# Hybrid SSD and chunk-MLP block on one core: four small products and a hold issued later, residual additions on VectorE, and another order of the last tiles

## The chip, the cores and the metric

The kernel runs on 1 core of one Trainium2 chip. The metric is the device time in microseconds of one execution. A core has TensorE (PE, matrix products into PSUM), VectorE (DVE), ScalarE (ACT), GpSimd (POOL) and SyncE (SP), whose queue issues the DMA transfers. Each engine works through its own instructions in the order in which the program issued them, and waits on semaphores for what others produce.

## What is computed

One transformer-like block on 1152 rows of width 1024: 1024 rows of one prompt and 128 rows of eight running streams. In the reference, cut to what matters here:

```python
h = rms_norm(x, norm_g[0]) * (1 + sc1) + sh1
z, xbc, dt_raw, uv = jnp.split(h @ w_in, ...)
xbc_act = silu(causal_conv(xbc))              # split into xs, B, C
dt = softplus(dt_raw + dt_bias)
y = ssd_scan(xs, dt, A, B, C, h0) + d_skip * xs
y_ssd = rms_norm(y * silu(z))
u, v = split(gelu(uv)); v = layer_norm(v)
y_cmlp = u * (tril(w_s) @ v + b_s)            # chunks of 128 rows
m = concat(y_ssd, y_cmlp) @ w_out
x = x + g1 * rms_norm(m, norm_g[1])
h = rms_norm(x, norm_g[2]) * (1 + sc2) + sh2
f = square(relu(h @ w_ff1)) @ w_ff2
x = x + g2 * rms_norm(f, norm_g[3])
```

All of it is in float32, and states and caches are returned too.

## The kernel before

The 1152 rows are nine tiles of 128 rows (t = 0 to 8), in three groups of three (g = 0, 1, 2; GT = 3, GW = 384 rows). Float32 products are made of three passes: each operand is split into a high part (a cast) and a low part (a subtraction). A split is a cast on ScalarE (L238, L258) or VectorE (L240) and a subtraction on VectorE (L241, L259); weights are split by a cast (L317, L319) and a subtraction L326 on GpSimd or VectorE, and the low part is kept in DRAM (`kl`) and loaded again as `wl` for later groups.

The mixer goes through the groups in order. `prep1_task(g)` loads x in natural and in transposed form, takes the sum of squares, scales the transposed tile by r (a small product `pr`, L506, spreads r over the partitions; L507 multiplies), modulates it (L427 on ScalarE; L433 and L434 on VectorE for tile 8) and splits it into `hT`. `m_in(g)` then runs the input projection: eight column tiles `xbc_0` to `xbc_7` with the convolution behind each (L632 to L656), then z in two halves (`pz0`, `pz1`), u in four column tiles (`pu_0` to `pu_3`) and v in two halves (`pv0`, `pv1`). `m_out(g)` is the output projection (`wo`, L1006 to L1009), and `out_task(g)` puts the residual on M, tile by tile. `ssd_task(g)` is the scan: gates of dt (L764 to L790, ending in `dA`), a prefix product `pa` (L797), its negative `nac` on VectorE (L805) and the transpose `pn` (L813), from which `rr` is built (L825), and per tile `px`, `pbn`, `par` (L859 to L879), the decays L (L892), `yd`, `yo`, `su` (L897 to L912). The MLP follows: `prep2_first` and others scale M by r (L456, L470), transpose it (`pt`, L252) and split it; then come the first products, with W made of sums of weights and of activations, and the long second product from 600 us to the end.

What sets the order is written out by hand. `m_in` and `m_out` are the main sequence; the small tasks are Python generators that stand in lanes. A lane runs one task at a time, in the order in which they were added. Each time the main sequence has issued some matmuls, it advances a model clock by their estimated ns, and a task goes on when the wait that it last gave has run out on that clock. These waits are the table WAIT: `dA0` is the wait of group 0 ahead of `pa`, `yd0` that ahead of `yd`, `prep1_tr1` and `prep1_tr2` those of groups 1 and 2 ahead of the first `pr`. `finish(task)` issues all that is left of a task before the main sequence goes on. `prep1_task(g)` waits for another task ahead of its first write to `hT`; for g = 2 that is `ssd_task(1)`:

```python
            if tl == 0:
                while not after.done:
                    yield
                new_hT(g)
```

In `m_in`, `ssd_task(g)` is added to lane A behind pz0. In `out_task` the tile's M is multiplied by r and the gate on VectorE (L1043) and the residual is added by `eng("xr")`, GpSimd (L1044). In `m_f2` the last pass ends with a loop over the three last tiles (L1704 on): per tile the rest of the product, a sum (L1713), ScalarE's square of one half (`fin_half`, L1633), the sum of both halves (L1637, `fin_r`) and r on GpSimd, then the product with r and gate (`fin_mul`, L1645), the addition to `x1l` (`fin_add`, L1651) and the store.

Of the kernel before, what the change touches and what calls it, by code (L numbers as in the profile page):

```python
# [19 lines left out]
D = 1024  # L20
KD = 8
NT = 9
GT = 3
# [18 lines left out]
def shape_constants():  # L42
# [14 lines left out]


WAIT = dict(
    L=12100, L0=3200, L1=0, L2=400, dA=28300, dA0=2400, dA1=2800, dA2=3200, evac=4100, gs1=4100, h0=4100, ln=5900,  # L60
    ln0=7300, ln1=9100, ln2=10000, lnr=5600, lnr0=2800, lnr1=600, lnr2=2000, modB=3000, modC=7600, mod_gate=2000,
    mod_load=8200, mod_mt=2100, next8=0, nexttile=6700, nexttile0=800, nexttile1=2400, nexttile2=1900, pn=20800,
    pn0=1900, pn1=0, pn2=3800, prep1_load=17400, prep1_load1=1700, prep1_load2=3200, prep1_next=13800,
    prep1_next1=4400, prep1_next2=1000, prep1_norm=11500, prep1_norm1=3300, prep1_norm2=800, prep1_split=40000,
    prep1_split1=400, prep1_split2=1000, prep1_stat=6500, prep1_stat1=1000, prep1_stat2=0, prep1_tr=5600,
    prep1_tr1=0, prep1_tr2=3500, prep2_load=1700, prep2_load0=200, prep2_load1=1500, prep2_load2=3600,
    prep2_next=3200, prep2_next0=2800, prep2_next1=2500, prep2_next2=5000, prep2_norm=6200, prep2_norm0=4000,
    prep2_norm1=3500, prep2_norm2=5000, prep2_split=1700, prep2_split0=1200, prep2_split1=800, prep2_split2=1500,
    prep2_stat=9600, prep2_stat0=1500, prep2_stat1=2500, prep2_stat2=4500, rr=11700, rr0=800, rr1=13000, rr2=400,
    set_load=10000, set_pcc=0, set_pw=2900, sp=13000, sp0=800, sp1=500, sp2=1900, sp_mid=22500, sp_mid0=9600,  # L70
    sp_mid1=0, sp_mid2=1400, sz=20900, sz0=1300, sz1=800, sz2=0, x1=14700, x10=2500, x11=7200, x12=4700, xr=29300,
    xr0=3000, xr1=2600, xr2=2700, yT=45700, yT0=2500, yT1=5600, yT2=2800, yc=23700, yc0=15400, yc1=16900,
    yc2=9500, yd=400, yd0=4500, yd1=6000, yd2=4900, yo8=2500, yr=11700, yr0=200, yr1=0, yr2=1100)
ENG = dict(p1hi=1, p2hi=0, ychi=0, yc=1, xdt=1, xw=1, xnD=1, L0=0, L1=0, sp=0, vg=0, vb=1, xr=1, S=0, rr=0, sz=1)
LO_POOL = {0, 1, 6, 7, 8, 9, 10, 11, 12, 13, 14, 15, 16, 17, 18, 19, 20, 21, 22, 24, 25, 26, 27, 28, 31, 32, 33, 35, 36, 39, 40, 41, 42, 43, 44, 46, 52, 53, 54, 55, 56, 60, 63, 64, 66, 68, 70, 72, 73, 77, 79, 80, 83, 85, 87, 89, 90, 91, 92, 93, 94, 95, 96, 97, 98, 100, 102, 103}
LOADS = [
# [41 lines left out]
def tile_block(ctx, tc, io, out):  # L118
# [13 lines left out]
    def eng(key):  # L132
        return pool if ENG[key] else dve
# [57 lines left out]
    def finish(*tasks):  # L191
        for t in tasks:
            while not t.done:
                tick(500.0)
# [504 lines left out]
    def m_in(g, ct0=0):  # L699
        if g not in gA:  # L700
            new_gA(g)
        dtx[g] = const.tile([P, GT, 8], F32, tag="dtx", name=f"dtx{g}", bufs=2)
        yT[g] = [None, None]

        def ev_u(ct):
            return lambda a: gelu2(up[g][:, ct, :], a[:, 0:GW], GW, f"gu{g}{ct}")

        def ev_z(half):
            def f(tl, a):
                if half == 0:  # L710
                    dve.tensor_tensor(dtx[g][:, tl, :], a[:, 0:8], dtb, op=ALU.add)
                a = a[:, 8:264] if half == 0 else a[:, 0:256]
                th = gt(f"zt{g}{tl}{half}")
                act.activation(th, a, AF.Tanh, scale=0.5)
                dve.scalar_tensor_tensor(sz[g][:, tl, 256 * half:256 * half + 256], th, 1.0, a, op0=ALU.add, op1=ALU.mult)
                zdone[g] = tl + GT * half
            return f

        for ct in range(ct0, 8):
            yield from m_proj_b(g, f"xbc{g}_{ct}", lambda a, ct=ct: xbc_evac(g, ct, a))  # L720
        if g > 0:
            finish(*gm_tasks[g - 1])
        if g == 2:
            finish(*out_tasks[0], p0)
        sz[g] = fslot(1 + g % 2, [P, GT, 512], F32, f"sz{g}")
        up[g] = fslot(0, [P, 4, GW], F32, f"up{g}")
        yield from m_proj_a(g, 264, f"pz0{g}", ev_z(0))
        ssd_tasks[g] = laneA.add(ssd_task(g))
        yield from m_proj_a(g, 256, f"pz1{g}", ev_z(1))
        for ct in range(4):  # L730
            yield from m_proj_b(g, f"pu{g}_{ct}", ev_u(ct))
        if g > 0:
            finish(ssd_tasks[g - 1])
        finish((mod_tasks[g] if g < 2 else ssd_tasks[1]))
        vall = fslot(1 + (g + 1) % 2, [P, GT, 512], F32, f"vt{g}")
        yT[g][1] = slot(YB_SLOT[g], [P, 4, 2, GW], F32R, f"yTb{g}")
        gm_tasks[g] = []

        def ev_v0(tl, a):
            gelu2(vall[:, tl, 0:256], a[:, 0:256], 256, f"gv0{g}{tl}")  # L740

        def ev_v1(tl, a):
            gelu2(vall[:, tl, 256:512], a[:, 0:256], 256, f"gv1{g}{tl}",
                  lambda: gm_tasks[g].append(laneG[tl].add(gmlp_task(g, tl, vall[:, tl, :]))))

        yield from m_proj_a(g, 256, f"pv0{g}", ev_v0)
        yield from m_proj_a(g, 256, f"pv1{g}", ev_v1)
        flush()
# [272 lines left out]
    def out_task(g, sst, ready):  # L1021
# [17 lines left out]
        for tl in range(GT):  # L1039
# [1 line left out]
            gv = gs1 if t == 8 else gate[0]  # L1041
            m = M[g][:, tl, :]
            dve.scalar_tensor_tensor(m, m, r, gv, op0=ALU.mult, op1=ALU.mult)  # L1043
            eng("xr").tensor_tensor(m, m, xs[tl], op=ALU.add)  # L1044
            if tl + 1 < GT:
                while tl + 1 not in ready:
                    yield
# [633 lines left out]
    def m_f2():  # L1681
# [4 lines left out]
        for i, (an, bn, gn) in enumerate(PASSES):  # L1686
# [20 lines left out]
            if last:  # L1707
                f2_prep(len(jobs2))
                for t in range(GT):
# [3 lines left out]
                    dve.tensor_tensor(a, a, bank[t], op=ALU.add)  # L1713
                    if t == 0:
                        finish(ft, ft2)
                    r = fin_r(GT + t, [fin_half(GT + t, 0), half1[:, t:t + 1]])
                    if t < 2:
                        fin_mul(GT + t, r)
                        fin_add(GT + t, x1l[:, t, :], ((0, 512, dve), (512, D, dve)))
                    else:  # L1720
                        for c0, c1, e in ((0, 384, pool), (384, D, dve)):
                            fin_mul(GT + t, r, ((c0, c1),))
                            fin_add(GT + t, x1l[:, t, :], ((c0, c1, e),))
                    yield 3 * LAST * 230.0
                continue
            if i == 0:
# [89 lines left out]
```

## Time and profile before

| | |
|---|---|
| median of 3 runs | 1334.36 us (1334.32 to 1338.89) |
| the profiled execution | 1334.28 us, span 1332.1 us |
| TensorE (PE) busy | 1254.1 us, 94% |
| VectorE (DVE) busy | 833.4 us, 63% |
| ScalarE (ACT) busy | 629.6 us, 47% |
| GpSimd (POOL) busy | 238.6 us, 18% |
| mean granted TensorE clock | 0.976 of full speed |

The busy shares are averages over stages with different limits. A row of the waits view says how long an engine sat idle ahead of a line, in total, how often, the longest, and what ended it. The columns of the other views stand at their first group below.

### The profile page before, as it was taken

How to read it: one execution, taken by the hardware profiler on the slowest of the kernel's cores; microseconds unless marked ns; L12 is line 12 of the kernel's file. 1: busy time of each engine (PE TensorE's matmuls, PEld its weight loads, DVE VectorE, ACT ScalarE, POOL GpSimd, SP SyncE). 2: the span in 40 equal slices, each digit the busy share in tenths (PEclk: the TensorE clock that was granted, in tenths of full speed). 3: DMA queues.
4: the chain of work that ended last, by engine and by line, in shares of the span. 5: the costliest groups of instructions: out<-in, count | busy, mean ns of one | idle time of the engine just before them, and what ended most of it. 6: DMA issues, size and time to landing. Idle time of an engine off the chain costs nothing. (4 is left out here: it accounts for less than half of the span.)

```text
span 1332.1 us, 18561 instructions
## 1 busy us (share of the span) xinstructions
PE 1254.1 (94%) x6815; PEld 1115.8 (84%) x6815; DVE 833.4 (63%) x1309; ACT 629.6 (47%) x1184; POOL 238.6 (18%) x266
## 2 busy tenths in 40 slices
PE   6988879989979999889999999999999999999996
PEld 4967767878779977789999999999988888888875
DVE  5476789566673543799885467576555335337666
ACT  3445534355574523546755444445433334344551
POOL 0133575147330443330000000000000000000001
PEclk9999979999999999989999999999999999999998
DMA  9778546745776467848448976665898337345863
GB/s 348 260 257 307 184 130 235 258 159 190 279 279 237 170 228 261 324 155 281 152 150 279 325 254 216 228 225 187 289 344 314 135 133 270 135 171 200 325 228 126
DMA packets 107154, 307.31 MB, mean 231 GB/s; under 512 B 12052, under 2 KB 31636, under 8 KB 107064
## 3 DMA queue, kind: packets, MB, share of 16 engines
q1 hardware_dynamic: 106632, 304.52, 64.6%
q10 hardware_dynamic: 432, 1.62, 0.3%
q8 instruction: 53, 0.87, 0.3%
q14 instruction: 37, 0.30, 0.1%
HBM read 232.47 MB, written 73.62 MB: 230 GB/s over the span
## 5 line engine op out<-in xcount | busy, mean ns | idle before, releaser
L241 DVE TENSOR_TENSOR bs<-br,bs 128x512 fp32r<-128x512 f32 x128 | 85.9, 689 | 107.2 <-ACT bs L238 106.9
L238 ACT CAST bs<-br 128x512 fp32r<-128x512 f32 x128 | 77.5, 619 | 146.5 <-PE G L1679 87.9
L1677 PE MATMUL P<-bs,as 128*128 128x512 f32 x336 | 132.1, 393 | 1.1 <-DVE acc L1740 1.1
L1679 PE MATMUL P<-bs,as 128*128 128x512 f32 x336 | 132.0, 393 | 0.0
L1678 PE MATMUL P<-bs,as 128*128 128x512 f32 x336 | 131.7, 392 | 0.0
L245 POOL TENSOR_SCALAR fr<-fss 128x1 f32<-128x1 f32 x9 | 2.8, 314 | 649.4 <-DVE fss L1637 649.4
L241 DVE TENSOR_TENSOR as<-ar,as 128x1536 fp32r<-128x1536 f32 x44 | 77.0, 1757 | 46.5 <-ACT as L238 46.5
L238 ACT CAST as<-ar 128x1536 fp32r<-128x1536 f32 x44 | 64.8, 1478 | 50.3 <-DMA ar<-fdA 26.2
L326 POOL TENSOR_TENSOR wl<-wr,wh 128x1024 fp32r<-128x1024 f32 (+1 forms) x28 | 70.3, 2514 | 86.7 <-ACT wh L319 52.1
L1677 PEld LDWEIGHTS P<-bs,as 128*128 128x128 f32 x336 | 63.1, 188 | 16.4 <-DVE acc L1740 2.0
L1678 PE MATMUL G<-bs,as 128*128 128x512 f32 x192 | 75.3, 392 | 0.0
L1677 PE MATMUL G<-bs,as 128*128 128x512 f32 x192 | 75.2, 392 | 0.0
L1679 PE MATMUL G<-bs,as 128*128 128x512 f32 x192 | 75.2, 392 | 0.0
L1679 PEld LDWEIGHTS P<-bs,as 128*128 128x128 f32 x336 | 63.1, 188 | 14.4
L1678 PEld LDWEIGHTS P<-bs,as 128*128 128x128 f32 x336 | 63.1, 188 | 14.2
L317 ACT CAST wh<-wr 128x1024 fp32r<-128x1024 f32 (+1 forms) x44 | 46.1, 1050 | 44.7 <-PE wo L1007 29.1
L652 DVE SCALAR_TENSOR_TENSOR cva<-pre,cwh,cva 128x256 f32<-128x256 f32 (+1 forms) x78 | 47.7, 653 | 12.4 <-ACT pre L634 11.5
L609 PE MATMUL xbc<-hT,wh 128*128 128x384 f32 x144 | 52.3, 363 | 0.0
L610 PE MATMUL xbc<-hT,wh 128*128 128x384 f32 x144 | 50.7, 352 | 0.0
L1447 DVE TENSOR_TENSOR wt<-wt 128x512 f32<-128x512 f32 x16 | 11.0, 689 | 51.6 <-DMA wt<-in_w_ff_dram 25.0
L1678 PEld LDWEIGHTS G<-bs,as 128*128 128x128 f32 x192 | 36.0, 188 | 8.2
L1677 PEld LDWEIGHTS G<-bs,as 128*128 128x128 f32 x192 | 36.0, 188 | 8.1
(938 smaller groups left out, 3674.0 us busy)
## 6 DMA issues: line engine op xcount, KB each, us to landing
wf<-in_w_f_dram SPq DMA_DIRECT2D x54, 512.0 KB, 4.8
wl<-kl SPq DMA_DIRECT2D x42, 512.0 KB, 4.2
wt<-in_w_ff_dram SPq DMA_DIRECT2D x16, 1024.0 KB, 6.3
td<-wt SPq DMA_DIRECT2D x64, 256.0 KB, 2.9
br<-in_w_ff_dram SPq DMA_DIRECT2D x32, 512.0 KB, 4.6
br<-td SPq DMA_DIRECT2D x32, 512.0 KB, 4.4
kl<-wl SPq DMA_DIRECT2D x26, 512.0 KB, 6.7
wr<-in_w_o_dram SPq DMA_DIRECT2D x24, 512.0 KB, 5.5
```

The costliest lines, as they stand in the source:

```text
L238: act.copy(hi, src)
L241: dve.tensor_tensor(lo, src, hi.bitcast(F32), op=ALU.subtract)
L245: pool.tensor_scalar(r, ss, 1.0 / n, eps, op0=ALU.mult, op1=ALU.add)
L317: act.copy(hi, raw)
L326: (pool if i in LO_POOL else dve).tensor_tensor(lo, raw, hi.bitcast(F32), op=ALU.subtract)
L609: pe.matmul(o, wh[:, k, :], x[:, 0, :], start=k == 0, stop=False)
L610: pe.matmul(o, wh[:, k, :], x[:, 1, :], start=False, stop=False)
L652: dve.scalar_tensor_tensor(dst, tap, w(k), dst, op0=ALU.mult, op1=ALU.add)
L1447: dve.tensor_tensor(b11, b12, b11, op=ALU.subtract)
L1677: pe.matmul(bank, x[:, 0], b[:, 0], start=first, stop=False, skip_group_check=True)
L1678: pe.matmul(bank, x[:, 0], b[:, 1], start=False, stop=False, skip_group_check=True)
L1679: pe.matmul(bank, x[:, 1], b[:, 0], start=False, stop=last, skip_group_check=True)
```

## The change

It does four things. Four entries of WAIT grow: `dA0` from 2400 to 6300, `yd0` from 4500 to 8500, `prep1_tr1` from 0 to 3000 and `prep1_tr2` from 3500 to 6000. In `m_in(2)` the `finish` of group 0's `out_task` and of `p0` (`prep2_first`) is moved from ahead of z to behind pz0. In `out_task` the residual addition of groups 1 and 2 is on VectorE. And in the last tiles both halves of acc are multiplied by the gate ahead of r; behind r one instruction per half multiplies by r and adds to `x1l`, all of it on VectorE.

```diff
-    ... dA=28300, dA0=2400, ...
+    ... dA=28300, dA0=6300, ...
-    prep1_tr1=0, prep1_tr2=3500, ...
+    prep1_tr1=3000, prep1_tr2=6000, ...
-    yc2=9500, yd=400, yd0=4500, ...
+    yc2=9500, yd=400, yd0=8500, ...
@@ m_in
         if g > 0:
             finish(*gm_tasks[g - 1])
-        if g == 2:
-            finish(*out_tasks[0], p0)
         sz[g] = fslot(1 + g % 2, [P, GT, 512], F32, f"sz{g}")
         up[g] = fslot(0, [P, 4, GW], F32, f"up{g}")
         yield from m_proj_a(g, 264, f"pz0{g}", ev_z(0))
+        if g == 2:
+            finish(*out_tasks[0], p0)
         ssd_tasks[g] = laneA.add(ssd_task(g))
@@ out_task
-            eng("xr").tensor_tensor(m, m, xs[tl], op=ALU.add)
+            (pool if g == 0 else dve).tensor_tensor(m, m, xs[tl], op=ALU.add)
@@ m_f2
-                    r = fin_r(GT + t, [fin_half(GT + t, 0), half1[:, t:t + 1]])
-                    if t < 2:
-                        fin_mul(GT + t, r)
-                        fin_add(GT + t, x1l[:, t, :], ((0, 512, dve), (512, D, dve)))
-                    else:
-                        for c0, c1, e in ((0, 384, pool), (384, D, dve)):
-                            fin_mul(GT + t, r, ((c0, c1),))
-                            fin_add(GT + t, x1l[:, t, :], ((c0, c1, e),))
+                    ss = [fin_half(GT + t, 0), half1[:, t:t + 1]]
+                    for cc in (lo, hi):
+                        dve.tensor_tensor(acc[1][:, t, cc], acc[1][:, t, cc], gate[1][:, cc], op=ALU.mult)
+                    r = fin_r(GT + t, ss)
+                    for cc in (lo, hi):
+                        dve.scalar_tensor_tensor(x1l[:, t, cc], acc[1][:, t, cc], r, x1l[:, t, cc], op0=ALU.mult,
+                                                 op1=ALU.add)
+                        load(out=yout(GT + t)[:, cc], in_=x1l[:, t, cc])
```

The four waits move many rows of the mixer. Three places are shown. The first is TensorE's order where group 0's output projection (`wo`) ends and `xbc_0` of group 2 begins; `pr` is the small product that spreads r of a tile of group 2, and the two shown are the second and the third. Rows of `wo` are left out at "...". Before, 66 rows stand between the second `pr` and `xbc_0`:

```order
L506 MATMUL pr_3215<-cs,r_3089 128x128
L1006 MATMUL wo_3059<-wh_3068,yTb_1221 128x512
...
L506 MATMUL pr_3261<-cs,r_3112 128x128
L1006 MATMUL wo_3264<-wh_3125,yTa_1245 128x512
...
L1009 MATMUL wo_3264<-wl_3278,yTb_1221 128x512 x2
L609 MATMUL xbc_0_3382<-hT_3198,wh_3307 128x384
```

And in the change, where 21 are left:

```order
L506 MATMUL pr_3299<-cs,r_3021 128x128
L1006 MATMUL wo_3231<-wh_3210,yTb_1221 128x512
...
L506 MATMUL pr_3350<-cs,r_3063 128x128
L1006 MATMUL wo_3231<-wh_3240,yTb_1221 128x512
...
L1009 MATMUL wo_3231<-wl_3241,yTb_1221 128x512 x2
L609 MATMUL xbc_0_3374<-hT_3285,wh_3273 128x384
```

Both `pr` moved some 45 rows towards `xbc_0`. On VectorE, between the product with the second `pr` and the last split of `hT` (L241), the change has these rows (`yTb` is the split of the gMLP output of group 1, which stood behind `hT` before):

```order
L507 TENSOR_TENSOR xT_3066<-xT_3066,pr_3299 128x1024
L240 CAST yTb_2597<-vt_2596 128x4x128
L241 TENSOR_TENSOR yTb_2597<-vt_2596,yTb_2597 128x4x128
L241 TENSOR_TENSOR hT_3285<-xT_3066,hT_3285 128x4x128
L241 TENSOR_TENSOR hT_3286<-xT_3066,hT_3286 128x4x128
...
L507 TENSOR_TENSOR xT_3291<-xT_3291,pr_3350 128x1024
...
L433 TENSOR_TENSOR xT_3291<-xT_3291,mod_G_108 128x512
L434 TENSOR_TENSOR xT_3291<-xT_3291,mod_sh_107 128x512
...
L241 TENSOR_TENSOR hT_3285<-xT_3291,hT_3285 128x4x128
L241 TENSOR_TENSOR hT_3286<-xT_3291,hT_3286 128x4x128
```

Three pairs L240 and L241 of `yTb` now lie among the rows that `xbc_0` needs.

The third place is TensorE between the u and v columns of group 1. Before, `pa` and `pn` of group 1's scan stand in `pu_0` and `pu_1`, and behind `pu_3` its tiles follow:

```order
L616 MATMUL pu_3_2541<-hT_1142,wl_2449 128x384 x4
L859 MATMUL px_2577<-cs,gA_1508 128x128 x4
L866 MATMUL pbn_2584<-cs,gA_1508 128x128 x2
L868 MATMUL pbn_2584<-gA_1508 128x128 x2
L879 MATMUL par_2592<-rr_2474,lt_2467 128x512
```

In the change:

```order
L616 MATMUL pu_3_2487<-hT_1142,wl_2394 128x384 x4
L797 MATMUL pa_2550<-dA_2548,cs 128x24
L798 MATMUL pa_2550<-dA_2548,nones 128x24
L384 MATMUL pm_2563<-modC_1492,cT 32x512 x4
L813 MATMUL pn_2569<-cs,nac_2556 128x128
L252 MATMUL mt_2585<-cs,modC_1492 128x128 x4
L587 MATMUL pv_0_2604<-wh_2437,hT_1141 128x256
```

The scan of group 1 starts behind `pu_3` there, and its tiles spread over `pv` and into `wo` of group 0.

## Rows read from the trace of the kernel before

**Rows 1.** the page's part 1, busy time, share of the span and instructions

```profile
PE 1254.1 (94%) x6815; PEld 1115.8 (84%) x6815; DVE 833.4 (63%) x1309; ACT 629.6 (47%) x1184; POOL 238.6 (18%) x266
```

**Rows 2.** TensorE's waits: line, what ended them, us in total, times, longest

```profile
PE pt L252 <- DVE M L470: 7.2, 4, 3.5
PE yd L897 <- DVE L L892: 7.2, 6, 4.4
...
PE pr L506 <- POOL r L246: 5.3, 2, 2.9
PE W L1406 <- DVE op2A L1359: 4.1, 1, 4.1
PE pa L797 <- DVE dA L790: 3.9, 1, 3.9
PE pt L252 <- DVE M L456: 3.7, 2, 2.0
PE xbc L616 <- DMA wl<-kl: 3.0, 1, 3.0
```

**Rows 3.** stretches: span, busy PE, PEld, DVE, ACT, POOL, granted clock, DMA

```profile
145.90:149.20 3.30, 3.30 (x12) 3.18 (x12) 2.44 (x8) 1.57 (x7) 0.89 (x3) 0.50 0.96 359
173.20:186.70 13.50, 10.62 (x38) 9.47 (x38) 11.01 (x12) 2.04 (x4) 9.81 (x7) 0.50 0.32 119
...
398.50:405.20 6.70, 5.50 (x25) 5.50 (x26) 1.20 (x4) 4.26 (x10) 0.00 (x0) 0.50 0.28 116
```

**Rows 4.** the same view by stage, of three stages

```profile
141.40:189.00 47.60, 34.75 (x179) 31.67 (x179) 38.67 (x55) 15.86 (x36) 30.06 (x28) 0.82 0.44 146
...
267.40:320.00 52.60, 49.04 (x328) 42.91 (x327) 36.67 (x61) 27.81 (x54) 28.27 (x28) 1.00 0.45 163
...
560.00:600.00 40.00, 33.61 (x172) 31.50 (x171) 36.10 (x51) 21.05 (x47) 11.93 (x12) 0.91 0.52 163
```

**Rows 5.** VectorE's timeline, 160 to 182 us: start, us, line, tiles

```profile
164.75 2.74 DVE L678 TENSOR_TENSOR vt<-vt,vg 128x512 f32<-128x512 f32 x1
167.41 3.61 DVE L652 SCALAR_TENSOR_TENSOR cva<-pre,cwh,cva 128x384 f32<-128x384 f32 x3
```

**Rows 6.** VectorE's timeline, gates of group 1's scan, first and last of 18

```profile
244.85 0.17 DVE L764 TENSOR_SCALAR ab<-dtx 128x24 f32<-128x24 f32 x1
...
249.73 0.18 DVE L790 TENSOR_TENSOR dA<-dt,acol 128x24 f32<-128x24 f32 x1
```

**Rows 7.** TensorE's timeline, two rows of wo with 18 matmuls from one to other

```profile
337.17 0.39 PE L1006 MATMUL wo<-wh,yTa 128*128 128x512 f32 x1
...
341.34 0.39 PE L1006 MATMUL wo<-wh,yTb 128*128 128x512 f32 x1
```

**Rows 8.** VectorE's and ScalarE's timeline, last tiles of prep1(2)

```profile
335.74 3.20 ACT L427 ACTIVATE xT<-xT,mod_sh,mod_G 128x128 f32<-128x128 f32 x8 [1.60 <-DVE xT L507]
...
339.78 1.14 ACT L238 CAST hT<-xT 128x512 fp32r<-128x512 f32 x2
...
343.75 1.21 DVE L507 TENSOR_TENSOR xT<-xT,pr 128x1024 f32<-128x1024 f32 x1
...
348.62 1.47 DVE L241 TENSOR_TENSOR hT<-xT,hT 128x512 fp32r<-128x512 f32 x2
350.00 0.42 DVE L240 CAST yTb<-vt 128x512 fp32r<-128x512 f32 x1
```

**Rows 9.** POOL's and VectorE's timeline, residual addition of tile 6

```profile
571.74 2.39 POOL L1044 TENSOR_TENSOR M<-M,xr 128x1024 f32<-128x1024 f32 x1 [9.35 <-DVE M L1043]
...
571.90 2.52 DVE L241 TENSOR_TENSOR h2T<-M,h2T 128x256 fp32r<-128x256 f32 x1
...
574.65 0.42 DVE L241 TENSOR_TENSOR h2T<-M,h2T 128x256 fp32r<-128x256 f32 x1
```

**Rows 10.** VectorE's timeline, last tiles, first row of two tiles

```profile
1312.78 0.69 DVE L1713 TENSOR_TENSOR acc<-acc,P 128x512 f32<-128x512 f32 x1 [1.75 <-PE P L1679]
...
1317.98 0.68 DVE L1713 TENSOR_TENSOR acc<-acc,P 128x512 f32<-128x512 f32 x1
```

More of the change, by code (lines that the diff above doesn't have):

```diff
@@ L59 @@
 WAIT = dict(
-    L=12100, L0=3200, L1=0, L2=400, dA=28300, dA0=2400, dA1=2800, dA2=3200, evac=4100, gs1=4100, h0=4100, ln=5900,
+    L=12100, L0=3200, L1=0, L2=400, dA=28300, dA0=6300, dA1=2800, dA2=3200, evac=4100, gs1=4100, h0=4100, ln=5900,
     ln0=7300, ln1=9100, ln2=10000, lnr=5600, lnr0=2800, lnr1=600, lnr2=2000, modB=3000, modC=7600, mod_gate=2000,
@@ L65 @@
     prep1_split1=400, prep1_split2=1000, prep1_stat=6500, prep1_stat1=1000, prep1_stat2=0, prep1_tr=5600,
-    prep1_tr1=0, prep1_tr2=3500, prep2_load=1700, prep2_load0=200, prep2_load1=1500, prep2_load2=3600,
+    prep1_tr1=3000, prep1_tr2=6000, prep2_load=1700, prep2_load0=200, prep2_load1=1500, prep2_load2=3600,
     prep2_next=3200, prep2_next0=2800, prep2_next1=2500, prep2_next2=5000, prep2_norm=6200, prep2_norm0=4000,
@@ L72 @@
     xr0=3000, xr1=2600, xr2=2700, yT=45700, yT0=2500, yT1=5600, yT2=2800, yc=23700, yc0=15400, yc1=16900,
-    yc2=9500, yd=400, yd0=4500, yd1=6000, yd2=4900, yo8=2500, yr=11700, yr0=200, yr1=0, yr2=1100)
+    yc2=9500, yd=400, yd0=8500, yd1=6000, yd2=4900, yo8=2500, yr=11700, yr0=200, yr1=0, yr2=1100)
 ENG = dict(p1hi=1, p2hi=0, ychi=0, yc=1, xdt=1, xw=1, xnD=1, L0=0, L1=0, sp=0, vg=0, vb=1, xr=1, S=0, rr=0, sz=1)
```

## The prediction, as it was put on record before the change ran

> **What bounds the kernel.** I read the page's busy shares first, then TensorE's waits grouped by what ended them, then TensorE's rows beside those of VectorE and GpSimd at each place that the change touches. TensorE is busy for 94% of the span [rows 1], and every later stage takes its output, so time is won only where it idles or runs at a low clock. The waits list names places: the transposes of M behind VectorE's L470 (7.2 us, the longest 3.5), yd behind L892 (7.2, longest 4.4), pr behind GpSimd's r (5.3, longest 2.9), W behind op2A (4.1), pa behind dA (3.9), pt behind L456 (3.7), xbc behind a weight load (3.0) [rows 2]. Nearly all stand between 86 and 600 us; the long product from 600 us on hardly waits. A wait has a second price: in the stretches after pa, after yd and after the hold ahead of z the granted clock is 0.50, the 1.2 GHz level instead of 2.4 [rows 3]. The engine had idled just before each of them. A stretch of 3.3 us at half clock costs half its work, 1.65 us, which I add to any TensorE wait of 2 us or more.
>
> The sum is made against the profiled execution, 1334.28 us (span 1332.1), which is the median of the runs, 1334.36, to 0.1 us.
>
> **A. First pr of group 1 (prep1_tr1).** It moves from the middle of pu_0 to its end, behind four pm rows and 16 matmuls, so r is there when it is reached. Removed: the 2.9 us wait [rows 2] and 1.7 of clock. **−4.6**. L507 and the modulation behind it have 24 matmuls of pu_1 and more as cover before hT of group 1 is asked for.
>
> **B. pa and yd of group 0 (dA0, yd0).** The pa row moves past the 24 matmuls of xbc_0, and the yd rows two column tiles on. Between 141.4 and 189 us TensorE works 34.75 of 47.6 us [rows 4]: 12.9 idle. Of the 13.5 us at half clock behind yd 10.62 are busy, so 5.3 are lost, and 1.65 behind pa [rows 3]; some 20 us are at stake. They don't all go. In VectorE's order nac (L805) now stands behind L677, L678, a statistics pair and three conv rows L652, which it did not before, and pn in xbc_1 needs it. Such an L678 took 2.74 us and such a triple of L652 3.61 in that stretch [rows 5]; their 6.3 us are the nearest price, so I put the wait at pn at 6 and add 3 of clock. What mix and su wait for, 2.9 us with 2.5 of clock, is VectorE's own backlog (38.67 busy of 47.6) and stays. 20 less 9 less 5.4 is 5.6: **−6**; from −12 (pn in time) to +2 (the backlog takes all back).
>
> **C. Group 1's scan, next in the same lane, starts later.** A lane runs one task at a time, so ssd_task(1) begins when ssd_task(0) has ended. Its gates were issued before pu_1, with pu_0 as cover; now they stand behind pu_3, and pa is the first row behind it, with only pm, pn and mt left until pv_0. VectorE's gate rows run from 244.85 to 249.91 [rows 6], 5.1 us, and the last gelu row before them takes another 0.5 behind pu_3; the new wait at pa is about 5.4, at pn and mt together 1.1, and 1.7 of clock: 8.2. The stretch from 267.4 to 320 us works 49.04 of 52.6 us [rows 4]: 3.6 us of short waits among the scan's rows, nearly all (I take 3.3) at this place, go with the rows that moved away. Net **+4.9**; 0 if the gates are picked up earlier than the order suggests, +9 if those short waits come again at pv.
>
> **D. First pr of group 2 (prep1_tr2).** It moved too; its 2.4 us (the rest of the 5.3 of [rows 2]) and 1.7 of clock go. **−4.1**.
>
> **E. Entry into group 2.** This is the bill for C and D. prep1(2) may write hT only when ssd_task(1) is done, so the second and third pr fall from 66 and 50 rows ahead of xbc_0 to 21 and 5. Behind the second pr 24 matmuls of wo remain; 18 of them take 4.17 us [rows 7], so the cover is 5.6. The chain that must end first: pr 0.4, L507 1.2, L427 3.2, the copies L238 0.6 and a wait for ScalarE's other rows 1.5, two L241 1.5, one pair L240 and L241 1.1, L507 1.2, another such pair 1.1, four L433/L434 (of L241's shape, 0.7 each) 2.8, L238 0.6, L241 0.7 [rows 8]. That is 16 us; with L241 at the longer times that it has beside GpSimd's wl it is 19. The wait at xbc_0 is 10.4 to 13; I take 11.2 and 3 of clock: **+14.2**; from +9.7 to +20.
>
> **F. What that wait gives back.** Weight loads for group 2 go on while TensorE stands. The wait of xbc for wl, 3.0 with 1.7 of clock, should vanish, and half of the 2.0 at L456 with 0.9 of clock. **−6.6**; nothing if these loads are themselves pushed back on SP's queue, where group 2's residual loads now come behind the weights.
>
> **G. The hold ahead of z.** `finish(*out_tasks[0], p0)` forced the last transposes of M out before pz0. After the change only one of three stands behind pz0's first half and two behind its second half; L470 is done by then. The 3.5 us [rows 2] and half of the 5.50 busy us at half clock [rows 3] go. **−6.2**. The slots of sz and up are taken earlier by this, but pz0's evacuation, which writes them first, stands where it stood.
>
> **H. Residual additions on VectorE.** Six 128x1024 additions leave GpSimd, where one takes 2.39 us, for VectorE, where a row of the same shape (L507) takes 1.21 [rows 8, 9]. Beside the GpSimd row an L241 of 128x256 takes 2.52 us, and 0.42 alone [rows 9]: 2.1 us come back for 1.2 spent. The Trainium skill, page "SBUF — State Buffer", section "Who interferes with whom", explains such a pair by a port that only one of the two can hold; the trace agrees, 2.52 against 0.42. Per tile VectorE gains 0.9 us, and r for the next tile isn't queued behind the addition on GpSimd. Of the 4.1 us wait at W and a 1.7 us one near 543 I let 2.5 go: **−2.5**, from −6 to +3.
>
> **I. Tail.** Now 5.20 us lie from one tile's L1713 to the next [rows 10]. The gate product is taken out of the chain behind r, but it overwrites what ScalarE's square still reads, so it waits for that, and the sum row L1637 is issued behind it. What is won behind r is lost ahead of it; the last tile saves 0.3 by having no slow GpSimd part. **−0.3**.
>
> Sum: −4.6 −6 +4.9 −4.1 +14.2 −6.6 −6.2 −2.5 −0.3 = −11.2. **1334.28 − 11.2 = 1323.** A measurement of this kernel tells about 0.5% (6.7 us) from no change.
>
> **Rivals.**
> 1. *The late scan costs more than the waits it removes* (slower). E at +20 and C at +9, with F at nothing and B at −2: −4.6 −2 +9 −4.1 +20 −6.2 −2.5 −0.3 = +9.3, **1343.6**. One mechanism: the lane delays ssd_task(1), and that delays hT(2). It decides once C and E together pass 26.4. For it: the order, in which every row between the second pr and xbc_0 stands on a chain. Against: E's own rows reach 13 us of wait, and a TensorE that stands still lets the loads catch up.
> 2. *VectorE bounds the stretch from 141 us on.* It is busy 38.67 of 47.6 us there, more than TensorE [rows 4]. Then the waits only change their names: B is 0 and all else stays, −11.2 + 6 = −5.2, **1329**, no difference. Against: pa waited for one short chain, not for a full engine.
> 3. *The moved waits go and no new ones come* (C 0, E +4): −26.3, **1308**. Against: E's chain is counted from rows.
> 4. *The additions make VectorE late for W.* Between 560 and 600 us it is busy 36.10 of 40 us [rows 4], and three additions of 1.21 us are added on its queue ahead of op2A, with the contention given back elsewhere. H becomes +3: **1328.6**. The Trainium skill, page "Perfetto Trace Analysis", section "Optimizing Scalar/DVE Operations", says that with VectorE saturated work may be moved off it to GpSimd, the contrary of this change; it also says that the two share a port, so that it might not help. By the first half of that rule the change loses here, by the second it doesn't; [rows 9] bear out the second.
>
> **Chances.** The forecast 0.47, rival 1 0.13, rival 2 0.14, rival 3 0.15, rival 4 0.11. Faster by over 0.5%: 0.47 + 0.15 = 0.62; no difference: 0.14 + 0.11 = 0.25; slower: 0.13. The range runs from rival 3 (1309) to just short of rival 1's price (1341), and leaves out half of rival 3 and most of rival 1.
>
> **What would show it.** Right: in TensorE's waits pr, dA's 3.9 and L470's 3.5 gone; a new wait of 10 us or more ahead of xbc_0 of group 2 behind L241, one of 5 at group 1's pa, one of 5 to 7 at pn; no GpSimd L1044 after 400 us, and L241 near 575 at 0.4; the tail's tile pace still 5.2. It is wrong if xbc_0 of group 2 doesn't wait (rival 3), if it waits 18 or more and wl waits remain (rival 1), if TensorE's idle time from 141 to 189 us is as before (rival 2), or if W waits longer than 4.1 (rival 4).

## The result, and the profile after

The change took **1344.01 us** (median of 6 runs, 1341.29 to 1348.83), the kernel before, on the same chip, 1335.55 (6 runs): ratio 1.0055, 95% interval 1.0036 to 1.0074. It is slower, by about the 0.5% that this kernel's measurement can tell. The forecast of 1323 had the wrong sign and its range ended at 1341; rival 1, the late scan, had been priced at 1343.6. (Of e20 in the table further below, one of ten executions took 1415 us at a granted clock of 0.836; its ratio leaves this one out.)

The profiled execution took 1341.29 us (span 1339.5). Of the page of the change, part 1, which answers to [rows 1]:

```profile
PE 1248.9 (93%) x6815; PEld 1112.1 (83%) x6815; DVE 837.1 (62%) x1316; ACT 631.6 (47%) x1184; POOL 222.5 (17%) x259
```

TensorE does the same 6815 products and loads and is even busy 5.2 us less, and VectorE has only 3.7 us more. So TensorE's idle time grew by 12.6 us (from 78.0 to 90.6), and its waits name it (columns as in [rows 2]: total, times, longest):

```profile
PE xbc L609 <- ACT hT L238: 8.8, 1, 8.8
PE pn L813 <- DVE nac L805: 7.1, 1, 7.1
PE pbn L866 <- DVE modC L392: 6.8, 1, 6.8
...
PE pt L252 <- DVE M L456: 5.8, 2, 4.0
PE pa L797 <- DVE dA L790: 5.3, 1, 5.3
PE pm L384 <- DMA modB<-in_w_mod_dram: 4.0, 1, 4.0
...
PE W L1406 <- DVE op2A L1359: 4.0, 2, 3.3
PE pt L252 <- DVE M L470: 3.3, 3, 1.8
...
PE yT L252 <- DVE xn L848: 2.9, 2, 1.9
...
PE wo L1006 <- DVE vt L571: 2.4, 1, 2.4
```

Of [rows 2], pr, yd, the 3.9 at pa and the 3.5 behind L470 are gone, as the change meant. Five new waits of 4 us or more stand in their place (xbc, pn, pbn, pa and pm), and at two of them, pbn and pm, the prediction had named nothing.

Where the time went shows when the same product is found in both traces. This table holds start times of TensorE rows, read from its two timelines; "stands" is by how much the change is late there, "stage" what was added since the line above, "priced" the prediction's terms for that stage.

| TensorE row | before | after | stands | stage | priced |
|---|---|---|---|---|---|
| pz0 of group 0, first | 64.47 | 64.45 | 0 | | |
| v of group 0, second half | 126.44 | 129.09 | +2.7 | A +2.7 | −4.6 |
| pz1 of group 1 | 236.47 | 231.27 | −5.2 | B −7.9 | −6 |
| wo of group 0, last quarter | 341.34 | 347.36 | +6.0 | C, D +11.2 | +0.8 |
| xbc_1 of group 2 | 354.65 | 373.21 | +18.6 | E +12.5 | +14.2 |
| pz1 of group 2 | 411.93 | 421.64 | +9.7 | F, G −8.9 | −12.8 |
| W, first products | 564.18 | 575.35 | +11.2 | +1.5 | not priced |
| W, 64 products on | 606.96 | 615.70 | +8.7 | H −2.4 | −2.5 |
| last product rows | 1318.80 | 1326.63 | +7.8 | −0.9 | not priced |
| end of the span | 1332.1 | 1339.5 | +7.4 | I −0.4 | −0.3 |

E, H and I came out near their price. A missed by 7.3 us, B with C and D by 8.5 (+3.3 against −5.2), F with G by 3.9. Two of these figures hang on the pair of executions. A is +2.4 to +2.7 in the change, e1 and e11, but within 0.2 of before in e12 and e17, which have the first pr moved too: no gain in any of the five, and no loss in two. And B's stage, 110.0 us before, took 107.7 to 110.2 in e3, e4, e10 and e18, whose program is that of before up to there, so that some 2 us of B's −7.9 may be chance.

B and C must be read together, since rows cross from one into the other: the third tile of group 0's scan (16 yd, 4 yo and 4 su) and a yT of four lay ahead of pz1 of group 1 and lie behind it now. The two stages as windows, first of the change, then of the kernel before (columns as in [rows 4]):

```profile
129.09:231.27 102.18, 79.88 (x484) 72.48 (x483) 86.67 (x114) 43.43 (x93) 59.20 (x46) 0.87 0.60 204
231.27:347.36 116.09, 103.02 (x642) 89.84 (x640) 68.89 (x116) 53.26 (x104) 50.07 (x52) 0.94 0.57 197
```

```profile
126.44:236.47 110.03, 88.45 (x511) 79.02 (x510) 92.35 (x124) 46.99 (x99) 66.38 (x52) 0.88 0.56 188
236.47:341.34 104.87, 98.84 (x618) 85.74 (x617) 62.92 (x113) 54.28 (x111) 44.35 (x46) 0.98 0.58 210
```

In stage B TensorE works 8.6 us less, and its idle time (span less PE busy) is 22.3 us where it was 21.6. So no idle time was won there at all: the waits moved from pa and yd to pn and pbn, and the 7.9 us come from the rows that left and from rows that run faster. In C, where these rows arrive and two pr have left, TensorE works 4.2 us more (103.02 − 98.84); the four yo and the four su that moved take 1.08 and 1.03 us there and took 2.02 and 1.97 before. The idle time of C rose by 7.0, from 6.0 to 13.1. Over both stages TensorE works 4.4 us less and idles 7.8 us longer; the idle time is the loss.

What pbn waits for can be read from TensorE and VectorE of the change:

```profile
182.72 1.07 PE L384 MATMUL pm<-modC,cT 128*32 128x512 f32 x8
...
198.04 0.69 PE L866 MATMUL pbn<-cs,gA 128*128 128x128 f32 x2 [6.79 <-DVE modC L392]
```

```profile
193.50 3.88 DVE L652 SCALAR_TENSOR_TENSOR cva<-pre,cwh,cva 128x384 f32<-128x384 f32 x3 [0.71 <-ACT pre L634]
197.31 0.67 DVE L392 TENSOR_TENSOR modC<-modC,pm 128x512 f32<-128x512 f32 x1
```

The kernel keeps its small PSUM tiles (tag aux) in a pool of four buffers (L144), taken in turn. Behind this pm come yd, su and px, so pbn is the fourth tile after it and gets its buffer; it starts 0.06 us after L392, which adds pm to modC, has ended. L392 stands behind conv rows L652 on VectorE, and VectorE had been busy for 26.9 of the 27.4 us from 164.16 to 191.59. The wait at pn has the same cause: nac (L805) starts at 157.52, behind L677, L678, a statistics pair and three L652 (all from 150.73 to 156.81).

**Stage A.** Two rows of TensorE's timeline of the change, then the same pm of the kernel before (start, us, line, and in brackets the idle time ahead of it):

```profile
95.06 0.38 PE L506 MATMUL pr<-cs,r 128*128 128x128 f32 x2
...
100.89 3.09 PE L384 MATMUL pm<-modB,cT 128*32 128x512 f32 x8 [4.04 <-DMA modB<-in_w_mod_dram]
```

```profile
101.53 1.20 PE L384 MATMUL pm<-modB,cT 128*32 128x512 f32 x8
```

pr waits for nothing now. But the next pm needs a load of modB that is there at 100.89, and TensorE stops in front of it instead. Before, pr's 2.9 us had brought TensorE to that pm at 101.53, after the load. (The other 0.9 us of new idle time in the stage is a wait of pv for wl, at 125.66.)

**Stage E.** TensorE at the entry into group 2, and the chain in front of it on ScalarE and on VectorE:

```profile
355.49 0.38 PE L506 MATMUL pr<-cs,r 128*128 128x128 f32 x2
...
366.07 0.69 PE L609 MATMUL xbc<-hT,wh 128*128 128x384 f32 x1 [8.79 <-ACT hT L238]
367.35 0.69 PE L610 MATMUL xbc<-hT,wh 128*128 128x384 f32 x1 [0.59 <-DVE hT L241]
```

```profile
353.75 3.19 ACT L427 ACTIVATE xT<-xT,mod_sh,mod_G 128x128 f32<-128x128 f32 x8 [3.54 <-DVE xT L507]
...
365.40 0.62 ACT L238 CAST hT<-xT 128x512 fp32r<-128x512 f32 x1 [3.31 <-DVE xT L434]
```

```profile
361.76 1.22 DVE L507 TENSOR_TENSOR xT<-xT,pr 128x1024 f32<-128x1024 f32 x1
...
366.00 0.69 DVE L434 TENSOR_TENSOR xT<-xT,mod_sh 128x512 f32<-128x512 f32 x1
```

TensorE runs the third pr at 355.49, but L507 of the third tile starts only at 361.76, behind the second tile's L427, copies and splits. The chain from the second pr (351.08) to the product at 367.35 is 16 us, as priced, and the wait 8.8 + 0.6 = 9.4 against 11.2.

**Stages H and I.** VectorE's timeline, tile 6 and the last tiles:

```profile
582.86 1.23 DVE L1044 TENSOR_TENSOR M<-M,xr 128x1024 f32<-128x1024 f32 x1
...
584.33 0.43 DVE L241 TENSOR_TENSOR h2T<-M,h2T 128x256 fp32r<-128x256 f32 x1
```

```profile
1320.58 0.69 DVE L1713 TENSOR_TENSOR acc<-acc,P 128x512 f32<-128x512 f32 x1 [1.74 <-PE P L1679]
...
1325.78 0.68 DVE L1713 TENSOR_TENSOR acc<-acc,P 128x512 f32<-128x512 f32 x1
```

The addition takes 1.23 us on VectorE against 2.39 on GpSimd, and the L241 behind it 0.43 against 2.52 [rows 9]; the wait at W fell from 4.1 to 3.3. What the Trainium skill says of the shared port (page "SBUF — State Buffer", section "Who interferes with whom") is in agreement with the pair of numbers. The tail's pace is 1325.78 − 1320.58 = 5.20 us, as before [rows 10].

### The profile page after: what moved, and what is told of

It is laid out like the page before. It is cut to its first block, busy times and chain, and to the rows that moved or that the text cites. A ratio compares the mean times of both kernels' runs of the same rounds, so it can differ in the third digit from the quotient of the medians.

```text
span 1339.5 us, 18548 instructions
## 1 busy us (share of the span) xinstructions
PE 1248.9 (93%) x6815; PEld 1112.1 (83%) x6815; DVE 837.1 (62%) x1316; ACT 631.6 (47%) x1184; POOL 222.5 (17%) x259
## 4 chain that ended last, share of the span: by engine, by line
PE 70%; DVE 13%; DMA 5%; ACT 5%; POOL 3%; issue 3%; SPq 1%; DVEq 0%; POOLq 0%; ACTq 0%
PE P L1677 6%; PE P L1679 5%; PE P L1678 5%; PE G L1678 3%; PE G L1677 3%; PE G L1679 3%; PE W L1406 3%; PE W L1404 3%; PE W L1405 3%; DVE cva L652 3%; PE Y L1406 2%; PE Y L1405 2%; PE Y L1404 2%; PE wo L1006 2%; PE wo L1007 1%
## 5 line engine op out<-in xcount | busy, mean ns | idle before, releaser
L241 DVE TENSOR_TENSOR bs<-br,bs 128x512 fp32r<-128x512 f32 x128 | 86.1, 689 | 107.3 <-ACT bs L238 107.1
L241 DVE TENSOR_TENSOR as<-ar,as 128x1536 fp32r<-128x1536 f32 x44 | 77.0, 1757 | 46.9 <-ACT as L238 46.8
L326 POOL TENSOR_TENSOR wl<-wr,wh 128x1024 fp32r<-128x1024 f32 (+1 forms) x28 | 70.1, 2508 | 92.7 <-ACT wh L319 53.3
L1678 PEld LDWEIGHTS P<-bs,as 128*128 128x128 f32 x336 | 63.1, 188 | 14.2
L652 DVE SCALAR_TENSOR_TENSOR cva<-pre,cwh,cva 128x256 f32<-128x256 f32 (+1 forms) x78 | 57.7, 781 | 13.5 <-ACT pre L634 12.6
L609 PE MATMUL xbc<-hT,wh 128*128 128x384 f32 x144 | 53.6, 372 | 8.8 <-ACT hT L238 8.8
L610 PE MATMUL xbc<-hT,wh 128*128 128x384 f32 x144 | 52.2, 362 | 0.7 <-DVE hT L241 0.6
L1678 PEld LDWEIGHTS G<-bs,as 128*128 128x128 f32 x192 | 36.0, 188 | 8.2
L1679 PEld LDWEIGHTS G<-bs,as 128*128 128x128 f32 x192 | 36.0, 188 | 8.1
L1677 PEld LDWEIGHTS G<-bs,as 128*128 128x128 f32 x192 | 36.0, 188 | 8.1
```

Of the source, the lines that this page charges most:

```text
L241: dve.tensor_tensor(lo, src, hi.bitcast(F32), op=ALU.subtract)
L326: (pool if i in LO_POOL else dve).tensor_tensor(lo, raw, hi.bitcast(F32), op=ALU.subtract)
L609: pe.matmul(o, wh[:, k, :], x[:, 0, :], start=k == 0, stop=False)
L610: pe.matmul(o, wh[:, k, :], x[:, 1, :], start=False, stop=False)
L652: dve.scalar_tensor_tensor(dst, tap, w(k), dst, op0=ALU.mult, op1=ALU.add)
L1677: pe.matmul(bank, x[:, 0], b[:, 0], start=first, stop=False, skip_group_check=True)
```

## The experiments

The head of the program, up to the first z product, took from 64.5 to 69.4 us from one profiled execution to the next. "From z on" in what follows is the time from that product to the end of the span, against the same in the trace of before. It is good to some 2 us: by pz1 of group 1, ahead of anything that they change, e3, e4 and e10 are already 2.1, 2.4 and 1.4 us shorter than before. Medians and ratios are against runs of the kernel before on the same chip; it ran between 1334.6 and 1336.2.

| run | what it is | median us | ratio, 95% | from z on |
|---|---|---|---|---|
| e1 | change, pa and yd put back | 1334.04 | 0.9990 (0.9967 to 1.0013) | −3.1 |
| e5 | before, pa and yd moved | 1349.34 | 1.0116 (1.0085 to 1.0148) | +13.2 |
| e3 | before, hold moved | 1328.78 | 0.9947 (0.9926 to 0.9967) | −7.1 |
| e4 | before, additions on VectorE | 1332.31 | 0.9981 (0.9966 to 0.9996) | −3.6 |
| e10 | change without its four waits | 1328.81 | 0.9948 (0.9929 to 0.9966) | −7.2 |
| e11 | change, gates of group 1 early | 1344.48 | 1.0074 (1.0044 to 1.0104) | +9.4 |
| e12 | before, both pr moved | 1342.94 | 1.0068 (1.0045 to 1.0090) | +2.4 |
| e13 | e12, later loads of xT | 1338.14 | 1.0017 (0.9998 to 1.0037) | +4.3 |
| e15 | e10, pa moved | 1347.64 | 1.0082 (1.0057 to 1.0106) | +14.2 |
| e16 | e10, yd moved | 1348.80 | 1.0100 (1.0085 to 1.0115) | +13.0 |
| e20 | e15, later loads of xT | 1341.94 | 1.0043 (1.0021 to 1.0064) | +2.1 |
| e17 | change, tile 7 scaled early | 1343.61 | 1.0069 (1.0042 to 1.0096) | +7.0 |
| e18 | e10, tile 7 scaled early | 1336.25 | 1.0013 (0.9994 to 1.0032) | +2.1 |
| e19 | change, later loads of xT | 1347.80 | 1.0071 (1.0051 to 1.0092) | +10.5 |
| e21 | e10, later loads of xT | 1328.56 | 0.9940 (0.9917 to 0.9963) | −5.7 |

### Is it the late scan?

**e1** is the change with two numbers put back, **e5** the kernel before with these two alone (the same lines turned round):

```diff
-    dA0=6300, ... yd0=8500
+    dA0=2400, ... yd0=4500
```

> The change with dA0 and yd0 put back to 2400 and 4500; the two prep1_tr waits, the moved hold, the additions on VectorE and the tail stay. Late scan as the cause: the gates of group 1 are again in pu_0 and the second pr of group 2 again 56 rows ahead of xbc_0, so the waits at pn (7.1), pbn (6.8), pa (5.3) and xbc_0 (8.8) go; the rest of the change is worth -8 to -10, about 1325 (0.993). Rival, the later pr of groups 1 and 2 are the cause: still 1340 or more. A wait of pm for the modB load near 101 us stays in both (4 us).

> The kernel before with dA0 6300 and yd0 8500 alone. Late scan as the cause: +12 to +20, so 1347 to 1354, with waits of 7 at pn, 5 at pa and 9 or more at xbc_0 of group 2. Rival, the later pr are the cause: 1334 or less, since the waits at pa and yd (8.2 us) go and nothing comes.

e5 is 1.2% slower; e1 comes back to the time of before. TensorE's waits of e5 have the lines of xbc, pn, pbn and pa word for word as the change has them (8.8, 7.1, 6.8 and 5.3 us). So moving pa and yd is what makes the kernel slower. The waits at pa and xbc are the delay through the lane that rival 1 named; those at pn and pbn lie in group 0's own scan. But e1 should have kept every other gain and came out 9 us above the 1325 expected. Its waits tell why:

```profile
PE wo L1009 <- POOL wl L326: 5.1, 1, 5.1
...
PE xbc L616 <- DMA wl<-kl: 4.9, 2, 4.0
...
PE pm L384 <- DMA modB<-in_w_mod_dram: 3.8, 1, 3.8
```

Three waits for loaded data stand where the two waits for r have gone; only the second of them was there before, at 3.0 us.

### The parts without a wait

**e3** moves the hold alone, **e4** the additions alone, **e10** is the change with all four numbers put back (hold, additions and tail stay).

```diff
-        if g == 2:
-            finish(*out_tasks[0], p0)
         yield from m_proj_a(g, 264, f"pz0{g}", ev_z(0))
+        if g == 2:
+            finish(*out_tasks[0], p0)
```

```diff
-            eng("xr").tensor_tensor(m, m, xs[tl], op=ALU.add)
+            (pool if g == 0 else dve).tensor_tensor(m, m, xs[tl], op=ALU.add)
```

> The kernel before with only the hold ahead of z of group 2 moved behind pz0. As predicted: the 3.5 us wait at pt behind L470 and its clock go, -6, 1328. Rival, from the trace of the change, where a pt still waits 1.8 for L470 inside pz0: the wait is moved and only partly hidden, -3, 1331. Second rival: no gain, as the earlier transposes were off the path, 1334.

> The kernel before with the residual additions of groups 1 and 2 on VectorE alone. As predicted -2.5, 1332 (the stretch of W from 564 to 600 us shorter by 2 to 3). Rival 4 of the prediction: VectorE late for W, +3, 1337.

> The change without its four new waits: the moved hold, the additions on VectorE and the tail alone. If the waits are the whole loss, the three parts add up as they measured alone: -6.3 (hold), -2.4 (additions), -0.4 (tail), about 1325 (0.993). Rival, the parts hide each other's gain: -5 or less, 1329 or more.

By medians the hold alone gave −7.1 us where −6.2 was priced, the additions −3.5 against −2.5; counted in the traces from pz1 of group 1 on, −5.0 and −1.2. G and H were near their price. Whether they add can't be told: their ratios make 0.72% together, with an interval of some 0.25 to either side, and e10, which has both and the new tail, gained 0.52% with 0.19. Counted from pz1 of group 1 on, e10 gains 5.8 us, close to their sum. The tail was not run alone.

### The two pr

**e12** sets only the two numbers of pr in the kernel before. **e13** is e12 with each load of a transposed tile xT behind the first issued one tile later, behind the product L507 in front of it:

```diff
-    prep1_tr1=0, prep1_tr2=3500
+    prep1_tr1=3000, prep1_tr2=6000
```

```diff
-        nh = tr(1)
...
             dve.tensor_tensor(h, h, pr[:, 0:P]...)
+            if tl + 1 < GT:
+                nh = tr(tl + 1)
...
-            if tl == 0:
-                nh = tr(2)
```

> The kernel before with prep1_tr1 3000 and prep1_tr2 6000 alone. As predicted (A and D): -8.7, 1326. Rival, from the traces so far: both pr waits covered loads that come at fixed times; pm then waits 4 us for modB near 101 and wo 5 us for wl near 345, so +2.7 and +4, 1339 to 1341.

> As the kernel with both pr moved, and each load of a transposed x tile of prep1 issued one tile later, behind the product with pr, so that it no longer stands in SP's queue ahead of the modB load and of the kl stores while it waits for its buffer. If that queue holds the loads: the pm wait near 101 falls from 4 to under 2 and the wl wait near 345 from 5 to under 2, 3 to 8 less than the kernel with both pr moved alone. Rival, the loads themselves take that long: no difference to it beyond 1 us.

Removing both waits for r alone makes the kernel slower. For the second, TensorE's, SP's queue's and GpSimd's timeline of e12:

```profile
344.69 1.22 PE L1009 MATMUL wo<-wl,yTb 128*128 128x512 f32 x2 [5.04 <-POOL wl L326]
```

```profile
336.27 0.33 SPq L491 DMA_DIRECT2D xT<-in_x_t_dram  x1
336.65 0.43 SPq L332 DMA_DIRECT2D kl<-wl  x1
```

```profile
341.91 5.51 POOL L326 TENSOR_TENSOR wl<-wr,wh 128x1024 fp32r<-128x1024 f32 x2 [6.82 <-DMA kl<-wl]
```

wo waits for a weight piece wl that GpSimd makes (L326); GpSimd waits 6.8 us for its buffer, until an older wl has been stored (kl<-wl); that store stands on SP's queue behind the xT load of the third tile, which leaves at 336.27. In e13, with the xT load out of the way, the wait at wl fell from 5.0 to 1.2 us, and the median by 4.8; its profiled run (+4.3 from z on) does not show the gain, in part since v of group 0 waits 5.5 us for vt where e12 waits 2.8 (all runs with later loads have this wait). For the first pr the same edit brought nothing: pm still waits 2.5 us. SP's queue of the change shows where its load stands:

```profile
92.34 0.33 SPq L486 DMA_DIRECT2D x<-in_x_prompt_dram  x1
93.52 0.33 SPq L491 DMA_DIRECT2D xT<-in_x_t_dram  x1
93.94 0.86 SPq L373 DMA_DIRECT2D modB<-in_w_mod_dram  x2
```

The load goes into the buffer that the fourth pm has read by 88.2 us, but it leaves 5.8 us later, behind a load of x (L486) that waited for a buffer of its own, and behind the first xT. It leaves 29.5 us after the first z product in before, the change, e12 and e13 alike, since e13 holds back only the second and third xT. So its place in the queue is the likely cause here too, but no run moved that load of x.

### One scan wait at a time

**e15** is e10 with pa moved alone (dA0=6300), **e16** with yd moved alone (yd0=8500), **e20** is e15 with e13's later loads.

> The kernel with hold, additions and tail alone (1328.8) plus dA0 6300, without yd0 and the two prep1_tr. pa of group 1 then stands between pu_2 and pu_3 instead of behind pu_3, and the second pr of group 2 is 56 rows ahead of xbc_0 instead of 21. If the lateness of group 1's scan is the cause: no 9 us wait at xbc_0, little or no wait at pa, within 3 of 1328.8 or below it. Rival, any pa behind xbc_0 costs by its wait at pn (7.1): +5 or more, 1334.

> The same with yd0 8500 instead of dA0 6300. In its order pa of group 1 stands behind pu_3 and the second pr of group 2 26 rows ahead of xbc_0, as with both. If that lateness is the cause: a wait of 5 at pa and of 7 or more at xbc_0, +10 to +14, 1339 to 1343. Rival, it takes both waits: 1332 or less.

> The kernel with hold, additions, tail and dA0 6300 (1347.6), with the same later loads. In its trace no hT is waited for, but wl four times (3.6, 5.0, 1.0, 3.9), each behind a kl store that stood behind a load of transposed x. If SP's queue is that kernel's loss: the wl waits of 3.6 and 5.0 fall below 2, 8 to 14 less, 1334 to 1340. Rival, the shifted scan itself is late: less than 3.

Against e10 (−7.2 from z on) each alone costs 20 to 21 us, more than both together cost on the kernel before (e5, 13.2). In e15 I had expected no loss, and it has no wait at xbc for hT. SP's queue of e15 has a cause:

```profile
321.13 12.27 SPq L491 DMA_DIRECT2D xT<-in_x_t_dram  x2
333.45 0.42 SPq L332 DMA_DIRECT2D kl<-wl  x1
...
348.22 0.33 SPq L491 DMA_DIRECT2D xT<-in_x_t_dram  x1
348.60 0.43 SPq L332 DMA_DIRECT2D kl<-wl  x1
```

Two xT loads hold the queue for 12.27 us (3.85 in e10), the third leaves at 348.22, and the stores come right behind each. GpSimd and TensorE of e15, the first of two such pairs (the second: 6.3 and 5.0 us):

```profile
338.77 2.34 POOL L326 TENSOR_TENSOR wl<-wr,wh 128x1024 fp32r<-128x1024 f32 x1 [4.53 <-DMA kl<-wl]
```

```profile
341.17 1.22 PE L1009 MATMUL wo<-wl,yTa 128*128 128x512 f32 x2 [3.59 <-POOL wl L326]
```

e20 shows that the queue is one part of the loss: 3.6 and 5.0 are gone (0.8 is left), the stage from the second quarter of wo to xbc_0 of group 2 is 1.7 us shorter than before where e15 was 8.2 longer, and from z on +14.2 became +2.1. But the median fell by only 5.7, short of the 8 to 14 expected, and stays 13 us above e21, the same kernel with pa in its old place. Part of this rest is the shifted scan itself, the rival that e20 was run against: where the second quarter of wo begins, e15 is already 7.4 us late against before and e20 11.1 (3.3 of them at the vt wait of all runs with later loads), behind waits that both have, 6.6 at pn, 4.3 at yT, 2.9 and 3.1 at px. e16 lost 20 us where 10 to 14 were expected: it waits 5.8 at pbn, 3.0 at pa of group 1, 4.1 at mt, and 5.1 + 1.7 at xbc_0.

### Cover at pa, and the entry into group 2

**e11** takes group 1's gates out of the scan's lane into a lane of their own behind pz0, as early as before. **e17** is the change with the product and modulation of group 2's second tile put ahead of the hold on the scan, **e18** the same in e10. **e19** is the change with later xT loads, **e21** e10 with them.

```diff
+        if g == 1:
+            d1 = {}
+            gates1.extend([laneF.add(ssd_gates(1, d1)), d1])
```

```diff
         for tl in range(GT):
+            if not (g == 2 and tl == 1):
+                yield from scale(h, tl)
...
+            if g == 2 and tl == 0:
+                yield from scale(nh, 1)
```

> The change, with the gates of group 1's scan (L764 to L790) issued by a lane of their own behind pz0, as early as before the change, and only pa and what follows left in ssd_task(1). If the lane's delay exposes the gates: the 5.3 us wait at pa behind pu_3 and 2 to 3 of clock go, -5 to -8 against the change, 1336 to 1339. Rival, pa's wait only covers the next one (par and yd behind pv): less than 2 against the change.

> The change, with the product with pr and the modulation (L427) of group 2's second tile issued ahead of prep1(2)'s hold on ssd_task(1) instead of behind it; nothing else moves by hand. If the chain from the scan's end to hT bounds the entry into group 2: 4 to 5 us of it are taken out, the wait at xbc_0 falls from 9.4 to 4 or 5, 4 to 6 less than the change, 1338 to 1340. Rival, loads or the scan itself set that entry: less than 2.

> The same edit in the kernel with hold, additions and tail alone, where xbc_0 of group 2 hardly waits: no difference to its 1328.8 beyond 2 if the chain there is covered, as its trace says.

> The change with each load of a transposed x tile of prep1 issued one tile later. If its loss at the entry into group 2 comes over hT alone (the chain from the end of group 1's scan): no difference beyond 3, 1341 to 1347. If it comes over SP's queue as well, which such a load holds while it waits for its buffer: 5 or more less, 1339 or below.

> The kernel with hold, additions and tail alone (1328.8), with the same later loads: its wl waits are 1.5 at most, so within 2 of it by the queue theory; below 1326 only if the queue also costs where no wait shows it.

In e11 pa's 5.3 us wait vanished and others took its place (TensorE's waits of e11):

```profile
PE pn L824 <- DVE nac L816: 8.1, 2, 7.1
...
PE mt L253 <- DVE modC L393: 4.7, 1, 4.7
```

mt had waited 0.4; of pn's two waits the second, 1.0, is new. mt needs VectorE's last addition to modC (here L393), and with the gates out of the way that addition comes behind 3.5 us of rr (L836), ahead of which it stood in the change. The total is that of the change: the place behind pu_3 seems to have too few products to cover VectorE's rows, whichever of them TensorE asks for first.

In e17 the wait at xbc_0 fell from 9.4 to 7.3 us and stage E from 12.5 to 9.7: 2.8 won where 4 to 6 were expected, and no difference to the change in the total. In e18 the same edit cost 7.4 us against e10, where no difference beyond 2 was expected. Moving the scale early moved SP's queue too, with the third xT load at 344.46 (4.5 us later than in e10, counted from the first z product) and the stores behind it (GpSimd of e18):

```profile
350.18 2.84 POOL L326 TENSOR_TENSOR wl<-wr,wh 128x1024 fp32r<-128x1024 f32 x1 [9.96 <-DMA kl<-wl]
```

e19 shows the other side: in the change itself later loads don't help. Stage E stays at +12.1 and xbc_0 waits 8.1 us for hT. There the chain through hT is the bound, not the queue, though e17, which took the scale out of that chain, won only part of the wait. e21 is level with e10: where nothing is late, the later loads neither help nor harm.

The best versions are e3, e10 and e21, level at 1328.6 to 1328.8 and 0.5% faster than before; the moved hold alone does it.

## Why the prediction was wrong, step by step

- **A failed** (−4.6, measured +2.7). The step "Removed: the 2.9 us wait [rows 2] and 1.7 of clock" holds for pr, but the wait had covered the modB load for the next pm. 4.0 us and 1.7 of half clock came in its place (2.7 us of wait in e12 and e17, where the stage is level with before). The prediction looked at what pr waited for, not at what the row behind it would wait for.
- **B, C and D** (+3.3 against −5.2). The waits at pn (7.1, "5 to 7") and at pa of group 1 (5.3 against 5.4) came as named, the one at pn by luck in its terms: L678 took 0.69 us and not 2.74, and L677, the statistics pair and a wait of 0.7 for GpSimd, which had no price, made up for it. Two steps failed. B had no price for pbn, 6.8 us, and this takes back what B was to win. Idle time in the stage stayed, which is the outcome of rival 2, and its mechanism is there as well: in the 47.6 us from 144.1, which answer to 141.4 to 189 of before, VectorE is busy 42.5 us where it was 38.7 [rows 4], and both waits end on rows that stand in its queue. Its chance of 0.14 rested on pa having "waited for one short chain, not for a full engine"; pn and pbn waited for the full engine. And C let 3.3 us of short waits "go with the rows that moved away". In C's stage the change waits 2.4 us at wo behind vt, 1.6 at par, 1.9 and 1.0 at yT, 0.4 at pbn: 7.3 us in place of the 3.6 that the stage had besides pr. The scan's tiles have no better cover in pv and wo. This is the case that the prediction had set at the upper end of C, "+9 if those short waits come again at pv". D's 2.4 us did go; but in e12 a wait of 5.0 at wl comes back for it where nothing else is late.
- **E was right in mechanism and near in size** (+12.5 against +14.2).
- **F failed** (F and G −8.9 against −12.8). The xbc wait for wl went, but pt behind L456 rose from 2.0 to 4.0 us where F had it halved. These two waits trade places in the runs: L456 waits 1.4 us behind a wl wait of 4.0 (e12), 3.4 behind 1.8 (e3) and 4.8 behind none (e10). G's step was right: the 3.5 at the last transposes is gone. The 1.8 that still stands behind L470 in the change (at 408.36) is that of an earlier tile, which waited as long before (at 388.16).
- **H and I were near in size.** Of H's 2.4 us at W, 0.9 is idle time and 1.6 work at a higher clock (granted clock 0.92 before, 0.96 after); the 1.7 us wait near 543 did not shrink. Rival 4 came from the Trainium skill's advice to move work off a full VectorE onto GpSimd (page "Perfetto Trace Analysis", section "Optimizing Scalar/DVE Operations"). Here the contrary move did no harm: in the 40 us that answer to 560 to 600 of before, VectorE is busy 36.03 us with the additions on it, and was 36.10 without [rows 4]. The same section's remark on the shared port is what e4 bears out. The window of the change:

```profile
571.20:611.20 40.00, 34.49 (x185) 32.70 (x184) 36.03 (x59) 23.54 (x52) 3.91 (x9) 0.96 0.49 161
```

- **Rival 1** had the right time, 1343.6 against 1344.0, by luck: it had the right culprit (e1, e5), but not the right sum. It needed E at +20, and E was 12.5. A's change of sign and the waits that C and B had not priced made up the rest. Its condition, C and E together past 26.4, was not met either (B, C, D and E are +15.8), so its chance of 0.13 was too low for a reason it didn't name: terms A, B and D were gains only as long as nothing stood behind the wait that they removed.

What stays open: why e12's median is 7.5 us above before while its profiled run, its fastest, is only 2.4 later from z on; how much of e15's and e16's loss is the scan's own waits and how much SP's queue; and whether the load of x is what holds back modB.

## What to carry to other kernels

Before a wait is priced as a gain, look at the rows just behind it for what arrives late there: twice here a wait for r was the cover of a transfer, and its removal uncovered 4 to 5 us. A step held back in a lane holds back everything behind it in the lane, and it meets the other engines' queues at another place; pa alone or yd alone each cost some 20 us on e10. A tile that shares its buffers with other tasks waits for their readers too, as pbn did for modC. And a load that must wait for its buffer, in front of an in-order issue queue, holds the stores behind it: follow a late weight back through its producer to the queue before changing the order of the products.

## What was unexpected of the hardware

TensorE lost clock once in the change without having stopped. There the granted clock of 482.4 to 487 us is 0.65, so most of it at the 1.2 GHz level and not at 2.4, while TensorE is busy for all of it, and for all of the 12.4 us ahead of it (window of the change):

```profile
482.40:487.00 4.60, 4.60 (x24) 4.12 (x23) 4.46 (x9) 0.70 (x2) 4.05 (x7) 0.65 1.04 395
```

The rows ahead of it are 16 products of 64 columns (yd) and 16 of 8 columns (pel). From the latter on the times grow (the change, then the kernel before at the same place):

```profile
482.37 2.21 PE L943 MATMUL pel<-dA,cs 128*128 128x8 f32 x16
484.43 0.77 PE L1006 MATMUL wo<-wh,yTa 128*128 128x512 f32 x1
```

```profile
472.57 1.90 PE L943 MATMUL pel<-dA,cs 128*128 128x8 f32 x16
474.33 0.48 PE L1006 MATMUL wo<-wh,yTa 128*128 128x512 f32 x1
```

Before, the same 32 products passed at full clock. The change lost some 1.6 us here, about the +1.5 of the line "W, first products"; in e17 it is 7.2 us at 0.53, a loss of 3.4, which took back most of what its earlier scaling had won. Of the other profiled executions e16 and e20 show it too (2.17 and 2.21 us for the 16 pel), the other thirteen do not (1.90). No run here tells what decides it.
